# Decoder trunk on one core: the FFN up product with tokens stationary, its result turned by VectorE transposes and SBUF-to-SBUF DMAs

## The chip, the cores and the metric

One core of a Trainium2 chip. The metric is the device time of one execution in microseconds; the time before is the median of three runs.

## The reference

Two layers of a decoder trunk over 256 tokens and 2048 features, float32 throughout. Each layer has a mixer, a cross-attention and a gated convolutional FFN:

```
def conv_ffn(h, w_up, conv_w, conv_b, w_down):
    u = causal_dwconv(h @ w_up, conv_w) + conv_b
    g, val = jnp.split(u, 2, axis=-1)
    return (jax.nn.silu(g) * val) @ w_down

h = h + conv_ffn(rms_norm(h, norm_ffn[l]), ffn_w_up[l], ffn_conv[l], ffn_conv_b[l], ffn_w_down[l])
```

`w_up` is 2048 x 11264, the convolution is causal along the tokens with three taps per feature, `w_down` is 5632 x 2048. The change is in `h @ w_up` and in what reads it.

## The kernel before

Activations lie with features on the 128 partitions and tokens along the free axis. A float32 product is made of three passes of shortened parts: an operand x is held as a rounded part and the exact rest, `x[:, k % 2, 0, :]` and `x[:, k % 2, 1, :]`, and so are the weights; rounded times rounded, rounded times rest and rest times rounded are added up in PSUM.

Weights come in pieces of 128 x 1024 floats (`stream`, L142 to L157). SP's queue issues the load of a piece (`raw`, 4 slots), ACT rounds it (`wh`, L154), DVE subtracts to get the rest (`wl`, L155). `wh` and `wl` have 3 slots each (pool `wp`), so ACT can round a piece when PE has left the one three before it. All loads stand in SP's queue in the order of use. The scheduler of the language sets each engine's order; the instructions inside `high_priority` are moved ahead.

`wstat` (L159) keeps weights stationary. Per k and tile of 128 features it makes one matmul of 512 columns (rounded weights against both parts of x, side by side) and one of 256 (rest of the weights against the rounded part). A call for 256 features fills one PSUM tile of two banks (pool `pmm`, 2 tiles). `xstat` (L178) keeps tokens stationary: per k and block of 128 tokens three matmuls of 512 weight columns. Before the change it serves the mixer's token-major products and the value product of cross-attention (tile `vp`, L187 to L189).

`ffn_up` (L892) runs 44 calls of `wstat`, 256 features each: 128 of the gate and 128 of the value. Each result goes through `ffn_tile` (L876): `fold` adds the two halves (an ACT copy at L201, a DVE addition at L202), `by_row` multiplies with the row factor of the RMSNorm (L206), then per half one ACT scaling with bias (L885) and two DVE multiply-adds along the tokens for the convolution (L886, L887), SiLU (L888), the product (L889), and the split into rounded part and rest (L209, L210). The 22 operand tiles then feed the down product (tile `res`, `project_residual`, L725).

Of the kernel before, what the change touches and what calls it, by code (L numbers as in the profile page):

```python
# [47 lines left out]
# pieces of the main stream between dependent pieces of a background task  # L48
# [15 lines left out]
class Task:  # L64
    """Work cut into pieces, to be emitted between the products of the main stream."""
# [5 lines left out]
class Trunk:  # L71
    def __init__(self, ctx, tc, a):
        self.tc, self.nc, self.a = tc, tc.nc, a
        pool = lambda name, bufs, **kw: ctx.enter_context(tc.tile_pool(name=name, bufs=bufs, **kw))
        self.const = pool("const", 1)
        self.par = pool("par", 1)
        self.actp = pool("actp", 29)
        self.raw = pool("raw", 4)
        self.wp = pool("wp", 3)
        self.tmp = pool("tmp", 6)  # L80
        self.ev = pool("ev", 3)
        self.col = pool("col", 3)
        self.rb = pool("rb", 2)
        self.pmm = pool("pmm", 2, space=bass.MemoryType.PSUM)
        self.psm = pool("psm", 4, space=bass.MemoryType.PSUM)

        self.tasks = deque()

# [6 lines left out]
    def pump(self):  # L95
        """One piece of the first task that isn't waiting."""
        free = None
        for task in self.tasks:
            if not all(t.done for t in task.after):
                continue  # L100
            if task.wait > 0:
                task.wait -= 1
            elif free is None:
                free = task
        if free is not None:
            try:
                free.wait = (next(free.gen) or 1) - 1
            except StopIteration:
                free.done = True
                self.tasks.remove(free)  # L110
# [24 lines left out]
    def claim(self, *tiles):  # L135
        """Slots are given in the order of first writes: these tiles get theirs now."""
        for t in tiles:
            t = t.bitcast(F32) if t.dtype == F32R else t
            self.nc.gpsimd.memset(t[0:32, 0, 0:1] if len(t.shape) == 3 else t[0:32, 0, 0, 0:1], 0.0)

# [1 line left out]
    def stream(self, wd, gc, kt):  # L142
        """Weight pieces from DRAM, split into a rounded part and an exact rest."""
        nc = self.nc
        kp = 1024 // gc
        for k in range(kt):
            if k % kp == 0:
                n = min(kp, kt - k) * gc
                raw = self.raw.tile([P, 1024], F32, tag="raw", name="raw")
                wh = self.wp.tile([P, 1024], F32R, tag="wh", name="wh")  # L150
                wl = self.wp.tile([P, 1024], F32R, tag="wl", name="wl")
                nc.sync.dma_start(raw[:, :n], wd[:, k * gc:k * gc + n])
                with self.tc.high_priority(offset=WPRIO):
                    nc.scalar.copy(wh[:, :n], raw[:, :n])  # L154
                    nc.vector.tensor_tensor(wl[:, :n], raw[:, :n], wh.bitcast(F32)[:, :n], ALU.subtract)  # L155
            o = (k % kp) * gc
            yield k, wh[:, o:o + gc], wl[:, o:o + gc]  # L157

    def wstat(self, xs, wd, kt=KT, name="mm", n=2):  # L159
        """Weights stationary, n output tiles: [A|B] each, A+B the product."""  # L160
        nc = self.nc
        ps = self.pmm.tile([P, 2, 512], F32, tag="mm", name=name)
        for k, wh, wl in self.stream(wd, n * P, kt):
            x = xs(k // 2) if callable(xs) else xs[k // 2]
            xhl = x[:, k % 2, :, :].rearrange("p a t -> p (a t)")
            xh = x[:, k % 2, 0, :]
            for m in range(n):
                ms = slice(m * P, (m + 1) * P)
                if k < kt - 1:
                    nc.tensor.matmul(ps[:, m, :], lhsT=wh[:, ms], rhs=xhl, start=(k == 0), stop=False)  # L170
                    nc.tensor.matmul(ps[:, m, 0:T], lhsT=wl[:, ms], rhs=xh, start=False, stop=False)  # L171
                else:
                    nc.tensor.matmul(ps[:, m, 0:T], lhsT=wl[:, ms], rhs=xh, start=False, stop=False)
                    nc.tensor.matmul(ps[:, m, :], lhsT=wh[:, ms], rhs=xhl, start=False, stop=True)  # L174
            self.pump()
        return ps

    def xstat(self, xs, wd, gc=512, name="mm"):  # L178
        """Tokens stationary: [token block, gc] for both token blocks."""
        nc = self.nc  # L180
        ps = self.pmm.tile([P, 2, 512], F32, tag="mm", name=name)
        for k, wh, wl in self.stream(wd, gc, KT):
            x = xs(k // 2) if callable(xs) else xs[k // 2]
            for tb in range(2):
                ts = slice(tb * P, (tb + 1) * P)
                xh, xl = x[:, k % 2, 0, ts], x[:, k % 2, 1, ts]
                nc.tensor.matmul(ps[:, tb, :gc], lhsT=xh, rhs=wh, start=(k == 0), stop=False)  # L187
                nc.tensor.matmul(ps[:, tb, :gc], lhsT=xh, rhs=wl, start=False, stop=False)  # L188
                nc.tensor.matmul(ps[:, tb, :gc], lhsT=xl, rhs=wh, start=False, stop=(k == KT - 1))  # L189
                self.pump()  # L190
        return ps

# [1 line left out]
    def fold(self, ps, name="z", z=None):  # L194
        """A + B of two output tiles, in SBUF float32."""
# [21 lines left out]
    def prep(self, src, gcol, j, x):  # L217
        """Operand tile of gain * src; the row factor is applied to the products."""
# [8 lines left out]
    def squares(self, src, j, acc):  # L227
        """acc += the squares of a tile"""
# [10 lines left out]
    def rsqrt_cols(self, ss, n, scale, out):  # L239
        """out = 1 / sqrt(ss * scale + EPS): a bit estimate for the scaled sum, and two third-order steps  # L240
        y * (t * t - 10/3 * t + 5) with t = v * y * y, each 8/3 times the root; the scale takes that back."""
# [14 lines left out]
    def spread(self, ps, col):  # L256
        """Every partition of ps gets the column as a row."""
        self.nc.tensor.matmul(ps, lhsT=col.broadcast_to([P, P]), rhs=self.ident, start=True, stop=True)

    def row_factor(self, acc, name, wait=1, *after):  # L260
        """1 / rms of every token, as columns and as a row on every partition; ready when the task is done."""
# [108 lines left out]
    def gla(self, l, tok, kq, ready, o_sb):  # L370
        """Gated linear attention into o_sb [P value, head, T], normalised per head and token."""
# [31 lines left out]
        # scores between tokens s and t by the smallest aligned block that holds both, its middle  # L403
        # between them: the decay is split there, so that every exponent is at most 0
# [23 lines left out]
        def products(lv, ke, qe):  # L428
            """Of a level only the tokens t in the second halves of its blocks are taken."""
# [22 lines left out]
        # blocks of 128 and 256 tokens: keys carried to the end of their chunk, queries from the start  # L452
        # of theirs; over 256 also past the chunk that lies between
# [48 lines left out]
        # values by token, RMSNorm over the value dimension, features back on the partitions  # L502
# [30 lines left out]
    def rope(self, dst, src, cols, tb, n):  # L533
        """dst = rotated src * factor; n heads of 64, cols = (factor, -factor)."""
# [12 lines left out]
    def swa_keys(self, tok, kp, vp):  # L547
        """Keys, and values for the two key heads, each with the other head's half at zero."""
# [35 lines left out]
    def swa(self, g, n, qTs, kp, vp, out):  # L584
        """Eight heads, one block of tokens: tiles j of heads (4g + j, 8 + 4g + j); two operand tiles."""
# [120 lines left out]
    def gla_out(self, o_sb, zr, oa):  # L706
        """Operand of silu(zr) * o."""
# [7 lines left out]
    def conv(self, j, cc, ch, y):  # L715
        """Short convolution of the gated channels (without the output gate)."""
# [8 lines left out]
    def project_residual(self, xs, w, gcol, kt=KT, last=False):  # L725
        """h += product; the operand of the next stage follows tile by tile."""
# [22 lines left out]
    def memory_factor(self):  # L749
        """1 / rms of every memory token, as columns and as a row on every partition."""  # L750
# [126 lines left out]
    def ffn_tile(self, ps, j, rbc, x):  # L877
        nc = self.nc
        z = self.fold(ps)
        self.by_row(z, rbc)  # L880
# [11 lines left out]
    def ffn_up(self, l, xs, acc):  # L892
        out, wait = [], []
        _, rbc, rt = self.row_factor(acc, "rx", W["ss"])
        for j in range(FT):
            wait.append((self.wstat(xs, self.a["wu"][l, j], name="up"), j))
            if j == 0:
                continue
            self.until(rt)
            for ps, i in wait:  # L900
                if i % 2 == 0:
                    out.append(self.operand(f"a{i // 2}"))
                self.ffn_tile(ps, i, rbc, out[-1])
            wait = []
# [26 lines left out]
def _groups(w, gc):  # L931
    """[depth, K, N] -> [depth, N/gc, 128, (K/128) * gc]"""
# [5 lines left out]
def _fm(x):  # L938
    """[256, 2048] -> [8, 128, 2, 256], features on partitions"""
# [3 lines left out]
def _colmajor(v):  # L943
    """[..., n*128] -> [..., 128, n]"""
# [3 lines left out]
def _layout(inp):  # L948
# [21 lines left out]
    d["wu"] = _groups(inp["ffn_w_up"][:, :, pair], 256)  # L970
# [50 lines left out]
```

## Time and profile before

| | |
|---|---|
| median of 3 runs | 2933.92 us (2933.08 to 2934.96) |
| the profiled execution, first to last instruction | 2931.9 us |
| PE, DVE, ACT busy in it | 2902.8, 1941.1, 1503.1 us |
| up product of layer 0, first and last matmul start | 724.6 and 1222.3 us |
| granted clock of TensorE, mean | 0.997 of 2.4 GHz |

The profile shows one execution, with a span of 2931.9 us from its first to its last instruction; the runs' times also hold what lies around it and are 1.2 to 3.1 us longer. Times in the rows are microseconds from the span's start unless marked ns. PE is the matmul, PEld the load of the stationary operand, which runs beside it; a matmul's end is modelled, so the distance from start to start tells its cost. SPq is SP's queue, which only issues DMAs.

### The profile page before, as it was taken

The page shows a single profiled execution, that of the slowest core. Times are in us where ns is not written, and L with a number is a line of the kernel's source. Part 1 is how long each engine was busy: PE and PEld are TensorE (multiplying, and loading weights), DVE is VectorE, ACT ScalarE, POOL GpSimd, SP SyncE. Part 2 cuts the span into 40 slices and gives each one's busy share as a digit, 9 for nine tenths or more (in the row PEclk, how much of TensorE's full clock was granted, in tenths as well). Part 3 has the DMA queues.
Part 4 walks back from the last instruction along what each step waited for, and adds up shares of the span by engine and source line. Part 5 has one row for each costly group of instructions (what it writes and reads, how often), then busy time and mean ns, then how long its engine had stood idle before and what let it go on. Part 6 is the DMA issues. An engine that isn't in the chain of part 4 may idle for free.

```text
span 2931.9 us, 42865 instructions
## 1 busy us (share of the span) xinstructions
PE 2902.8 (99%) x16712; PEld 2523.1 (86%) x16712; DVE 1941.1 (66%) x2865; ACT 1503.1 (51%) x2117; POOL 28.6 (1%) x53
## 2 busy tenths in 40 slices
PE   7999999999999999999999999999999999999998
PEld 7888888888888888888898888888888888888887
DVE  7886665556777777655567866655567777776454
ACT  5565444444555555544455654444455555555443
POOL 3000000000000000000000000000000000000000
PEclk9999999999999999999999999999999999999999
DMA  6556565556556565666664566555555555566664
GB/s 193 156 172 207 189 186 167 165 171 187 184 184 189 184 188 186 191 187 190 183 182 144 166 193 188 186 162 169 174 186 186 187 185 189 184 189 188 188 187 144
DMA packets 148589, 530.32 MB, mean 181 GB/s; under 512 B 17152, under 2 KB 17696, under 8 KB 148384
## 3 DMA queue, kind: packets, MB, share of 16 engines
q1 hardware_dynamic: 148384, 527.57, 58.6%
q8 instruction: 131, 2.15, 0.3%
q14 instruction: 74, 0.61, 0.1%
HBM read 525.40 MB, written 2.10 MB: 180 GB/s over the span
## 4 chain that ended last, share of the span: by engine, by line
PE 98%; DVE 1%; issue 0%; DMA 0%; ACT 0%; SPq 0%; DVEq 0%; ACTq 0%
PE up L170 21%; PE res L170 19%; PE up L171 11%; PE res L171 9%; PE kp L170 4%; PE qp L170 4%; PE vp L188 2%; PE vp L187 2%; PE vp L189 2%; PE qp L171 2%; PE kp L171 2%; PE zc L170 2%; PE up L174 1%; PE zq L187 1%; PE zq L189 1%; PE zq L188 1%
## 5 line engine op out<-in xcount | busy, mean ns | idle before, releaser
L155 DVE TENSOR_TENSOR wl<-raw,wh 128x1024 fp32r<-128x1024 f32 (+2 forms) x993 | 1208.5, 1218 | 720.6 <-ACT wh L154 719.0
L154 ACT CAST wh<-raw 128x1024 fp32r<-128x1024 f32 (+2 forms) x993 | 1033.6, 1041 | 962.1 <-PE res L170 303.0
L170 PE MATMUL up<-xs,wh 128*128 128x512 f32 x2640 | 936.0, 398 | 0.0
L171 PE MATMUL up<-xs,wl 128*128 128x256 f32 x2640 | 741.9, 281 | 0.0
L170 PEld LDWEIGHTS up<-xs,wh 128*128 128x128 f32 x2640 | 496.1, 188 | 118.0
L171 PEld LDWEIGHTS up<-xs,wl 128*128 128x128 f32 x2640 | 498.8, 189 | 3.6
L170 PE MATMUL res<-a,wh 128*128 128x512 f32 x1376 | 482.6, 395 | 0.0
L171 PE MATMUL res<-a,wl 128*128 128x256 f32 x1376 | 385.9, 280 | 0.0
L170 PEld LDWEIGHTS res<-a,wh 128*128 128x128 f32 x1376 | 258.0, 187 | 60.1
L171 PEld LDWEIGHTS res<-a,wl 128*128 128x128 f32 x1376 | 260.0, 189 | 0.8
L170 PE MATMUL qp<-xs,wh 128*128 128x512 f32 x480 | 171.4, 397 | 0.0
L170 PE MATMUL res<-xo,wh 128*128 128x512 f32 x480 | 170.5, 398 | 0.0
L170 PE MATMUL kp<-ms,wh 128*128 128x512 f32 x480 | 169.5, 397 | 0.0
L171 PE MATMUL res<-xo,wl 128*128 128x256 f32 x480 | 134.9, 281 | 0.0
L171 PE MATMUL qp<-xs,wl 128*128 128x256 f32 x480 | 134.8, 281 | 0.0
L171 PE MATMUL kp<-ms,wl 128*128 128x256 f32 x480 | 134.6, 280 | 0.0
L201 ACT COPY z_b<-up 128x512 f32<-128x512 f32 x88 | 51.6, 587 | 161.3 <-PE up L174 161.3
L202 DVE TENSOR_TENSOR z<-up,z_b 128x512 f32<-128x512 f32 x88 | 60.9, 692 | 105.8 <-ACT z_b L201 105.8
L885 ACT ACTIVATE u<-z,par 128x256 f32<-128x256 f32 x176 | 96.6, 595 | 48.7 <-DVE z L206 48.7
L170 PEld LDWEIGHTS res<-xo,wh 128*128 128x128 f32 x480 | 90.2, 188 | 21.3
L170 PEld LDWEIGHTS kp<-ms,wh 128*128 128x128 f32 x480 | 90.1, 188 | 21.1
L170 PEld LDWEIGHTS qp<-xs,wh 128*128 128x128 f32 x480 | 90.1, 188 | 18.9
(316 smaller groups left out, 4145.3 us busy)
## 6 DMA issues: line engine op xcount, KB each, us to landing
raw<-in_wu SPq DMA_DIRECT2D x352, 512.0 KB, 4.5
raw<-in_wd SPq DMA_DIRECT2D x175, 512.0 KB, 3.6
raw<-in_w_fm SPq DMA_DIRECT2D x80, 512.0 KB, 4.3
raw<-in_wk SPq DMA_DIRECT2D x64, 512.0 KB, 4.8
raw<-in_wo SPq DMA_DIRECT2D x64, 512.0 KB, 4.4
raw<-in_wq SPq DMA_DIRECT2D x64, 512.0 KB, 4.0
raw<-in_wv SPq DMA_DIRECT2D x64, 512.0 KB, 3.6
raw<-in_wxo SPq DMA_DIRECT2D x64, 512.0 KB, 3.9
```

Source lines behind the costliest of these rows:

```text
L154: nc.scalar.copy(wh[:, :n], raw[:, :n])
L155: nc.vector.tensor_tensor(wl[:, :n], raw[:, :n], wh.bitcast(F32)[:, :n], ALU.subtract)
L170: nc.tensor.matmul(ps[:, m, :], lhsT=wh[:, ms], rhs=xhl, start=(k == 0), stop=False)
L171: nc.tensor.matmul(ps[:, m, 0:T], lhsT=wl[:, ms], rhs=xh, start=False, stop=False)
L174: nc.tensor.matmul(ps[:, m, :], lhsT=wh[:, ms], rhs=xhl, start=False, stop=True)
L187: nc.tensor.matmul(ps[:, tb, :gc], lhsT=xh, rhs=wh, start=(k == 0), stop=False)
L188: nc.tensor.matmul(ps[:, tb, :gc], lhsT=xh, rhs=wl, start=False, stop=False)
L189: nc.tensor.matmul(ps[:, tb, :gc], lhsT=xl, rhs=wh, start=False, stop=(k == KT - 1))
L201: nc.scalar.copy(b, ps[:, :, T:2 * T])
L202: nc.vector.tensor_tensor(z, ps[:, :, 0:T], b, ALU.add)
L885: nc.scalar.activation(u[:, s, :], z[:, s, :], AF.Identity, bias=self.p[:, C_FB + m:C_FB + m + 1], scale=tap[2])
```

## The change

`ffn_up` calls `xstat` instead of `wstat`, 512 features (two pairs of gate and value tiles) at a time: 22 calls a layer. With `striped=True` the stationary operand takes every second token, so that block tb holds tokens 2m + tb, and its elements lie 8 bytes apart. The result then has tokens on the partitions, and the new `turn` brings features back there: for each block a DVE transpose of 32 x 32 squares from PSUM into `zt`, then 16 DMAs of 32 partitions x 1 KB from `zt` to `zf`, all issued by SP. The row factor is multiplied in one DVE instruction of 1024 elements per partition that reads `zf` and writes back to `zt`; `fold` and `by_row` are no longer called here. `zt` and `zf` have two slots each; the scratch for dynamic DMAs is set to 1024, and `w_up` is laid out in groups of 512 columns.

```diff
+        self.turnp = pool("turnp", 2)
...
-    def xstat(self, xs, wd, gc=512, name="mm"):
+    def xstat(self, xs, wd, gc=512, name="mm", kt=KT, striped=False):
...
+                if striped:
+                    xh, xl = (x[:, k % 2, u, :].rearrange("p (m b) -> p b m", b=2)[:, tb, :] for u in range(2))
+                else:
+                    xh, xl = (x[:, k % 2, u, tb * P:(tb + 1) * P] for u in range(2))
...
+    def turn(self, ps, name="z"):
+        nc = self.nc
+        zt = self.turnp.tile([P, 4, 4, 32, 2], F32, tag="zt", name=name + "_t")
+        zf = self.turnp.tile([P, 4, 4, 64], F32, tag="zf", name=name)
+        with self.tc.high_priority(offset=WPRIO):
+            for tb in range(2):
+                nc.vector.transpose(out=zt[:, :, :, :, tb].rearrange("p b k j -> p k b j"),
+                                    in_=ps[:, tb, :].rearrange("p (k b j) -> p k b j", k=4, b=4))
+            for a in range(4):
+                for b in range(4):
+                    nc.sync.dma_start(zf[32 * b:32 * b + 32, a].rearrange("p k u -> p (k u)"),
+                                      zt[32 * a:32 * a + 32, b].rearrange("p k j t -> p (k j t)"))
+        return zf, zt.rearrange("p b k j t -> p (b k j t)").rearrange("p (k t) -> p k t", k=4)
...
-    def ffn_tile(self, ps, j, rbc, x):
-        nc = self.nc
-        z = self.fold(ps)
-        self.by_row(z, rbc)
+    def ffn_tile(self, z, j, x):
+        nc = self.nc
...
-        for j in range(FT):
-            wait.append((self.wstat(xs, self.a["wu"][l, j], name="up"), j))
+        for j in range(0, FT, 2):
+            zf, z = self.turn(self.xstat(xs, self.a["wu"][l, j // 2], name="up", striped=True))
             if j == 0:
-                continue
-            self.until(rt)
+                self.until(rt)
+            nc.vector.tensor_tensor(z.rearrange("p k (a u) -> p k a u", a=4), zf.rearrange("p a k u -> p k a u"),
+                                    rbc.rearrange("p (a u) -> p a u", a=4).unsqueeze(1).broadcast_to([P, 4, 4, 64]),
+                                    ALU.mult)
+            out.append(self.operand(f"a{j // 2}"))
+            for i in range(2):
+                self.ffn_tile(z[:, 2 * i:2 * i + 2], j + i, out[-1])
```

The order on DVE in the middle of the up product. Before, one group of 256 features (four pieces; `wl` is the rest of a weight piece, `z` the folded result, `u` the convolution, `a` the operand of the down product):

```order
L202 TENSOR_TENSOR z<-up,z_b 128x512
L206 TENSOR_TENSOR z<-z,rxb 128x512
L155 TENSOR_TENSOR wl<-raw,wh 128x1024
L886 SCALAR_TENSOR_TENSOR u<-z,par,u 128x255 x2
L887 SCALAR_TENSOR_TENSOR u<-z,par,u 128x254 x2
L155 TENSOR_TENSOR wl<-raw,wh 128x1024
L889 TENSOR_TENSOR u<-u 128x256
L155 TENSOR_TENSOR wl<-raw,wh 128x1024
L210 TENSOR_TENSOR a_8095<-u,a_8095 128x256
L155 TENSOR_TENSOR wl<-raw,wh 128x1024
```

Now, from one turn on, one group of 512 features (eight pieces; `z_t` is `zt`, `z` is `zf`):

```order
L206 STREAM_TRANSPOSE z_t<-up 128x4x4x32 x2
L156 TENSOR_TENSOR wl<-raw,wh 128x1024 x4
L919 TENSOR_TENSOR z_t<-z,rxb 128x1024
L905 SCALAR_TENSOR_TENSOR u<-z_t,par,u 128x255 x2
L906 SCALAR_TENSOR_TENSOR u<-z_t,par,u 128x254
L905 SCALAR_TENSOR_TENSOR u<-z_t,par,u 128x255
L906 SCALAR_TENSOR_TENSOR u<-z_t,par,u 128x254
L905 SCALAR_TENSOR_TENSOR u<-z_t,par,u 128x255
L906 SCALAR_TENSOR_TENSOR u<-z_t,par,u 128x254
L156 TENSOR_TENSOR wl<-raw,wh 128x1024
L906 SCALAR_TENSOR_TENSOR u<-z_t,par,u 128x254
L156 TENSOR_TENSOR wl<-raw,wh 128x1024
```

The transposes stand right after the group's end, four rests of weight pieces follow, and then the row product, which waits for the 16 DMAs; seven multiply-adds stand between it and the next rest. The pieces of these rests, counted from the first of the finished group: 10 to 13 before the row product, 14 behind the seventh multiply-add.

The order in SP's queue at the head of layer 0's up product. Before:

```order
L152 DMA raw<-in_wv 128x1024 x32
L152 DMA raw<-in_wxo 128x1024 x32
L152 DMA raw<-in_wu 128x1024 x176
L152 DMA raw<-in_wd 128x1024 x82
L152 DMA raw<-in_wd 128x512
```

Now:

```order
L153 DMA raw<-in_wxo 128x1024 x32
L153 DMA raw<-in_wu 128x1024 x14
L210 DMA z<-z_t 32x256 x16
L153 DMA raw<-in_wu 128x1024 x8
L210 DMA z<-z_t 32x256 x16
L153 DMA raw<-in_wu 128x1024 x8
L210 DMA z<-z_t 32x256 x16
```

The 16 DMAs of a turn stand between the weight loads of pieces 13 and 14, counted as above; what SP issues behind them waits until they are issued.

## Rows read from the trace of the kernel before

**Rows 1.** The page's engines: busy us (share of the span) xinstructions.
```profile
PE 2902.8 (99%) x16712; PEld 2523.1 (86%) x16712; DVE 1941.1 (66%) x2865; ACT 1503.1 (51%) x2117; POOL 28.6 (1%) x53
```

**Rows 2.** The page's chain that ended last: shares of the span by engine.
```profile
PE 98%; DVE 1%; issue 0%; DMA 0%; ACT 0%; SPq 0%; DVEq 0%; ACTq 0%
```

**Rows 3.** Tile up, layer 0: duration ns min/median/max, first to last start us.
```profile
L170 PE MATMUL up<-xs,wh x1320: 387/398/481, 724.6 to 1221.5; 128*128 128x512 f32 x189
...
L174 PE MATMUL up<-xs,wh x88: 392/394/400, 735.8 to 1222.3; 128*128 128x512 f32 x88
```

**Rows 4.** Timeline of PE, a group's end: start us, duration us, instruction.
```profile
905.93 0.39 PE L174 MATMUL up<-xs,wh 128*128 128x512 f32 x1
906.16 0.39 PE L170 MATMUL up<-xs,wh 128*128 128x512 f32 x1
```

**Rows 5.** Timeline of ACT, the same group and the next; idle time before in brackets.
```profile
906.36 0.59 ACT L201 COPY z_b<-up 128x512 f32<-128x512 f32 x1 [1.90 <-PE up L174]
...
908.43 1.10 ACT L885 ACTIVATE u<-z,par 128x256 f32<-128x256 f32 x2 [0.54 <-DVE z L206]
...
917.66 0.59 ACT L201 COPY z_b<-up 128x512 f32<-128x512 f32 x1 [1.90 <-PE up L174]
```

**Rows 6.** Timeline of DVE, the same group.
```profile
907.70 0.69 DVE L206 TENSOR_TENSOR z<-z,rxb 128x512 f32<-128x512 f32 x1
908.31 1.22 DVE L155 TENSOR_TENSOR wl<-raw,wh 128x1024 fp32r<-128x1024 f32 x1
909.45 0.87 DVE L886 SCALAR_TENSOR_TENSOR u<-z,par,u 128x255 f32<-128x255 f32 x2
```

**Rows 7.** Timeline of PE in the value product, tokens stationary.
```profile
533.13 0.40 PE L188 MATMUL vp<-wl,ms 128*128 128x512 f32 x1
...
534.96 0.39 PE L187 MATMUL vp<-wh,ms 128*128 128x512 f32 x1
```

**Rows 8.** Timeline of ACT in the value product: first and last of four roundings.
```profile
571.31 1.05 ACT L154 CAST wh<-raw 128x1024 fp32r<-128x1024 f32 x1 [1.67 <-PE vp L189]
...
579.47 1.05 ACT L154 CAST wh<-raw 128x1024 fp32r<-128x1024 f32 x1 [1.67 <-PE vp L189]
```

**Rows 9.** Groups by line and shape, 747 to 1224 us: busy us, mean ns | idle before.
```profile
L155 DVE TENSOR_TENSOR wl<-raw,wh 128x1024 fp32r<-128x1024 f32 x169 | 206.3, 1221 | 70.4 <-ACT wh L154 70.4
L154 ACT CAST wh<-raw 128x1024 fp32r<-128x1024 f32 x169 | 176.9, 1047 | 89.6 <-PE up L170 89.6
L885 ACT ACTIVATE u<-z,par 128x256 f32<-128x256 f32 x84 | 46.1, 596 | 22.4 <-DVE z L206 22.4
```

**Rows 10.** Groups by line and shape on DVE, whole span.
```profile
L809 DVE TENSOR_REDUCE xac<-xs 128x2 f32<-128x512 f32 x8 | 5.5, 692 | 3.9 <-PE xs L803 3.9
...
L500 DVE COPY am<-att 64x512 f32<-64x512 f32 x2 | 0.8, 421 | 0.1
```

**Rows 11.** Timeline of SP's queue at the start: issues without a wait.
```profile
0.74 0.39 SPq L297 DMA_DIRECT2D gmix<-in_gmix  x1
...
2.12 0.43 SPq L152 DMA_DIRECT2D raw<-in_w_tok  x1
2.60 0.43 SPq L304 DMA_DIRECT2D h<-in_x  x1
...
4.02 0.43 SPq L152 DMA_DIRECT2D raw<-in_w_tok  x1
```

**Rows 12.** DMA issues: xcount, KB each, median us from issue to landing.
```profile
raw<-in_wu SPq DMA_DIRECT2D x352, 512.0 KB, 4.5
...
gmix<-in_gmix SPq DMA_DIRECT2D x1, 8.0 KB, 1.8
```

**Rows 13.** Tile out (256 KB each, SBUF to DRAM at the end): its DMAs.
```profile
DMA to landing us min/median/max: 2.0/2.4/2.6
```

**Rows 14.** Windows: stretch, us, busy us by engine, granted clock, DMA share, GB/s.
```profile
747.00:1224.00 477.00, 477.00 (x2704) 414.27 (x2703) 353.33 (x508) 270.04 (x381) 0.00 (x0) 1.00 0.60 187
```

**Rows 15.** Loads of the stationary operand in the value product, whole span.
```profile
L187 PEld LDWEIGHTS vp<-wh,ms 128*128 128x128 f32 x256 | 48.1, 188 | 9.4
```

More of the change, by code (lines that the diff above doesn't have):

```diff
@@ L176, in wstat @@
         return ps
-    def xstat(self, xs, wd, gc=512, name="mm"):
+    def xstat(self, xs, wd, gc=512, name="mm", kt=KT, striped=False):
         nc = self.nc
         ps = self.pmm.tile([P, 2, 512], F32, tag="mm", name=name)
-        for k, wh, wl in self.stream(wd, gc, KT):
+        for k, wh, wl in self.stream(wd, gc, kt):
             x = xs(k // 2) if callable(xs) else xs[k // 2]
             for tb in range(2):
-                ts = slice(tb * P, (tb + 1) * P)
-                xh, xl = x[:, k % 2, 0, ts], x[:, k % 2, 1, ts]
+                if striped:
+                    xh, xl = (x[:, k % 2, u, :].rearrange("p (m b) -> p b m", b=2)[:, tb, :] for u in range(2))
+                else:
+                    xh, xl = (x[:, k % 2, u, tb * P:(tb + 1) * P] for u in range(2))
                 nc.tensor.matmul(ps[:, tb, :gc], lhsT=xh, rhs=wh, start=(k == 0), stop=False)
                 nc.tensor.matmul(ps[:, tb, :gc], lhsT=xh, rhs=wl, start=False, stop=False)
-                nc.tensor.matmul(ps[:, tb, :gc], lhsT=xl, rhs=wh, start=False, stop=(k == KT - 1))
+                nc.tensor.matmul(ps[:, tb, :gc], lhsT=xl, rhs=wh, start=False, stop=(k == kt - 1))
                 self.pump()
         return ps
+    def turn(self, ps, name="z"):
[11 more added lines that the diff above has]
+        return zf, zt.rearrange("p b k j t -> p (b k j t)").rearrange("p (k t) -> p k t", k=4)
     def fold(self, ps, name="z", z=None):
@@ L892, in ffn_up @@
     def ffn_up(self, l, xs, acc):
-        out, wait = [], []
+        nc = self.nc
+        out = []
         _, rbc, rt = self.row_factor(acc, "rx", W["ss"])
-        for j in range(FT):
-            wait.append((self.wstat(xs, self.a["wu"][l, j], name="up"), j))
+        for j in range(0, FT, 2):
+            zf, z = self.turn(self.xstat(xs, self.a["wu"][l, j // 2], name="up", striped=True))
             if j == 0:
-                continue
-            self.until(rt)
[L900 to L904, printed above, removed]
+                self.until(rt)
[5 more added lines that the diff above has]
+                self.ffn_tile(z[:, 2 * i:2 * i + 2], j + i, out[-1])
         return out
@@ L969, in _layout @@
     pair = np.arange(2 * D_FF).reshape(2, FT, P).transpose(1, 0, 2).reshape(-1)
-    d["wu"] = _groups(inp["ffn_w_up"][:, :, pair], 256)
+    d["wu"] = _groups(inp["ffn_w_up"][:, :, pair], 512)
     d["x"], d["mem"] = _fm(inp["x"][0]), _fm(inp["mem"][0])
@@ L1009 @@
     arrays = _layout({n: np.asarray(v) for n, v in inputs.items()})
-    nc = bacc.Bacc("TRN2", target_bir_lowering=False, num_devices=1)
+    nc = bacc.Bacc("TRN2", target_bir_lowering=False, num_devices=1, dynamic_dma_scratch_size=1024)
     feeds, aps = {}, {}
```

## Prediction

> **What bounds the kernel now.** Read the engines' busy time first: TensorE (PE) is busy 99% of the span, VectorE (DVE) 66%, ScalarE (ACT) 51% [rows 1]. The chain of waits says the same: 98% of it is PE [rows 2]. So time can be won only by giving PE less to do, and lost by making it wait. The up product runs from 724.6 us to just after 1222.3 in layer 0 [rows 3] and as long in layer 1. Its group of 256 features ends every 11.30 us: ACT's copy of a finished group starts at 906.36 and the next at 917.66 [rows 5]. 44 groups take 44 x 11.30 = 497.2 us a layer. PE doesn't pause between groups [rows 4]; in the stretch DVE works 353 of 477 us and the DMA engines are busy 0.60 [rows 14], so both have room on average.
>
> **PE's own work.** The columns don't change: for 512 features and one k, 4 pairs of 512 + 256 before, 6 matmuls of 512 after, 3072 columns both times. The number of matmuls falls from 8 to 6, and each has a price of its own. The nearest rows of the new form are the value product of cross-attention, the same helper with tokens stationary: 8 matmuls start in 534.96 - 533.13 = 1.83 us [rows 7], and where nothing else is mixed in, a weight piece of two k (12 matmuls) takes (579.47 - 571.31) / 3 = 2.72 us [rows 8], 0.227 a matmul. Before, the same piece took 11.30 / 4 = 2.83 us. After: 22 groups x 8 pieces x 2.72 = 478.7 us a layer, 18.5 less; two layers give **-37 us**, if PE never waits.
>
> **What is taken off and put on beside PE.** Off, per 512 features: two ACT copies, two DVE folds and two row products (the last cost DVE 0.69 each in the timeline [rows 6]). On: two transposes out of PSUM, one product of 1024 elements, 16 DMAs on SP's queue. The taps, SiLU and splits stay. DVE's average load hardly moves, so I price none of this as throughput. What counts is the order in which DVE, ACT and SP wait.
>
> **The chain behind each turn.** Let t = 0 be the moment a group's last matmul gives way to the next (906.16 in [rows 4]); ACT follows 0.20 later [rows 5]. Call the finished group's pieces 0 to 7. There are three slots for the rounded part and three for the rest, so piece n is rounded only when PE has left piece n-3. DVE's order after the change is: two transposes, the rests of pieces 10 to 13, the row product, seven of the eight multiply-adds, the rest of piece 14. Two things must be there before the row product.
>
> - The rest of piece 13. PE leaves piece 10 at 3 x 2.72 = 8.16; +0.20, +1.05 for the rounding [rows 9], and 0.04 to hand over, as from DVE to ACT in [rows 5, 6]: it starts at 9.45. DVE's next instruction follows 1.14 later (908.31 to 909.45 [rows 6]): **10.59**.
> - The sixteenth DMA. No row shows a transpose. A read of 512 columns of PSUM by a one-source instruction took 692 ns, a copy of 512 in SBUF 421 ns [rows 10]; above, two passes would be 1.38 us. I take 0.69, as that row reads the same amount from the same memory. The second starts 0.61 after the first, as behind the 0.69 of [rows 6]; both are done at 0.20 + 0.61 + 0.69 = 1.50. SP's queue issues one DMA every (4.02 - 2.12) / 4 = 0.475 us when nothing holds it [rows 11]: the sixteenth starts at 1.55 + 15 x 0.475 = 8.67. No row shows a transfer from SBUF to SBUF. The nearest, 8 KB into an idle queue and 256 KB out of SBUF, land 1.8 and at least 2.0 us after issue [rows 12, 13]; 4.5 us, the weights' own time among each other [rows 12], is the upper end. I take 2.05, since by then SP has issued no weights for 8 us: 10.7, and with eight semaphores to pass **10.85**.
>
> So the row product starts at about 10.85 and ends 1.22 later (1024 elements, as the row of the same size [rows 9]), at 12.07. Then ACT starts 0.04 later and needs 0.60 for the first of four scalings and 0.51 for each further one [rows 5, 9], a multiply-add holds DVE 0.40 (two in 0.87 us [rows 6]). In the order given the seventh starts 3.15 after the product's end, piece 14's rest at 3.55, and it is there at 4.77: 16.84. PE wants it with its second matmul of piece 14, at 6 x 2.72 + 0.23 = 16.55; with 0.1 to hand over, **PE waits 0.4 us per group**. Without any late DMA it would be 0.1. The wait repeats after every group but the last of a layer, whose followers are the slower pieces of the down product: 42 x 0.4 = 17 us.
>
> The weights queued behind the 16 DMAs on SP have cover: piece 14 is issued at 8.67 + 0.475 = 9.15 and lands by 13.7 [rows 12], its rounding is due at 14.2. The start and the end of the stage cost nothing: the last operand of the down product is wanted only at its k = 42, some 29 us later.
>
> **A rule weighed against a row.** SP's row shows 0.43 us per issue and 0.475 from one to the next [rows 11], so 16 issues are 7.6 us and they are what makes the product late. The Trainium skill, DMA: Bandwidth & Descriptors, "Anatomy of one DMA", puts the sequencer's dispatch at about 50 ns, though for the GpSimd path. By that the sixteen would be out in an estimated 0.8 us, nothing would be late, and the time would be that of the second case below; I go by the row.
>
> **Sum.** -37 + 17 = **-20 us**. The profiled execution spans 2931.9 us, 2 below the median of the runs, 2933.9; from the median: **2914 us**.
>
> **The cases.** About 0.2% (6 us) is what a measurement of this kernel can tell from no change.
>
> 1. Forecast, the product 0.1 to 0.6 late: 2903 to 2928, chance 0.40.
> 2. Nothing late: transposes near 0.42, or a shorter issue for 32 partitions. For it: 16 transfers of 32 KB are small. Against: an issue of 8 KB holds SP 0.39 us, one of 256 KB 0.43 [rows 11]. -37 + 42 x 0.12 = -32: 2902, chance 0.18.
> 3. **A wait takes the place of the work removed, and more.** The place is DVE's row product, with piece 14's rest queued behind it. Each microsecond that it starts later costs PE 42 us. It decides against the change when the product starts after about 11.35 (a wait of 0.88 x 42 = 37). Transposes of 1.38 us put it at 12.2: 42 x 1.8 - 37 = +37, 2971. Landing at 3.2 instead of 2.05 puts it at 12.0: +28, 2962. For it: the spare time is under 0.5 us, and two unpriced operations stand in series. Against: each nearest row is well under these ends. Chance 0.34, a third of it within 0.2%.
> 4. **The stationary load becomes PE's pace.** Tokens are now taken every second element, 8 bytes apart. The packed load took 188 ns [rows 15], hidden under 227 ns. It decides from 227 ns: each further ns costs 4224 matmuls 4.2 us, and twice 188 would cost 4224 x 0.149 = +630 us. No row has a load with such a step. The Trainium skill, SBUF — State Buffer, "Door 1: The DMA port swizzle", says SBUF is read in lines of 16 bytes at full rate as long as two accesses fall in a line; a step of 8 bytes is just that, so by it this case doesn't come. No run here shows it. Chance 0.08.
>
> **How the numbers follow.** The likeliest is case 1. Cases 1 and 2 are faster, 0.57 with a little of the first lost to the middle; within 0.2% comes the middle of case 3, 0.12; slower 0.31. The range reaches from 2896, no wait at all, to 2965 in case 3; outside lie the ends of cases 3 and 4. Cases 1 and 2 alone would span 2896 to 2928.
>
> **What would show it.** In the changed profile: up matmuls 0.227 us apart and stationary loads at 188 ns (else case 4); sixteen SP issues spread over 7 us after each pair of transposes; the row product starting about 10.85 us after a group's end; one gap of some 0.4 us in PE per group, released by DVE's rest of the seventh piece of the next group. No gap means case 2; a gap over 0.88 makes the prediction's sign wrong. If the gap is released by ACT's rounding waiting for a weight DMA instead, the queue's cover was misjudged.

## The result, and the profile after

The changed kernel takes **3099.22 us** (3094.78 to 3100.68), against 2933.82 for the kernel before on the same chip: a ratio of 1.0562, 95% interval 1.055 to 1.0575. The forecast was 2914 with a range to 2965: the change costs time where a gain was expected, and the time lies 134 us above the range.

The profile of the changed kernel, its engines (answers to [rows 1]) and the chain that ended last (answers to [rows 2]), by engine and by line:

```profile
PE 2967.7 (96%) x15304; PEld 2508.6 (81%) x15304; DVE 1941.0 (63%) x2821; ACT 1450.8 (47%) x2029; POOL 29.3 (1%) x53
...
PE 70%; SPq 13%; DVE 9%; DMA 4%; issue 3%; ACT 1%; DVEq 0%; ACTq 0%
PE res L171 17%; SPq L210 13%; PE res L172 9%; PE kp L171 4%; PE qp L171 4%; PE up L192 3%; PE up L191 3%; PE up L193 3%; DVE wl L156 2%; DMA z<-z_t 2%; DVE u L905 2%; PE vp L192 2%; PE vp L191 2%; PE vp L193 2%; PE qp L172 2%
```

The chain was 98% PE and is now 70%. The largest share that isn't PE's is line 210 in SP's queue: issuing the turn's DMAs, 13%.

One group's end as the timeline shows it (start us, duration us, instruction, idle time before). Its last matmul starts at 901.39, so t = 0 of the prediction is 901.62. First SP's queue, then DVE, then ACT:

```profile
903.16 10.24 SPq L210 DMA_DIRECT2D z<-z_t  x16
913.50 14.52 SPq L153 DMA_DIRECT2D raw<-in_wu  x8
```

```profile
901.82 1.31 DVE L206 STREAM_TRANSPOSE z_t<-up 128x512 f32<-128x512 f32 x2
...
911.07 1.23 DVE L156 TENSOR_TENSOR wl<-raw,wh 128x1024 fp32r<-128x1024 f32 x1 [1.57 <-ACT wh L155]
914.87 1.23 DVE L919 TENSOR_TENSOR z_t<-z,rxb 128x1024 f32<-128x1024 f32 x1 [2.57 <-DMA z<-z_t]
...
919.63 1.22 DVE L156 TENSOR_TENSOR wl<-raw,wh 128x1024 fp32r<-128x1024 f32 x1
```

```profile
916.13 2.08 ACT L904 ACTIVATE u<-z_t,par 128x256 f32<-128x256 f32 x4 [5.09 <-DVE z_t L919]
918.12 1.98 ACT L155 CAST wh<-raw 128x1024 fp32r<-128x1024 f32 x2
```

The transposes start at 0.20 and are done at 1.51, SP issues from 1.54, the last of the 16 leaves at about 11.2, and the row product starts at 13.25 instead of 10.85. Behind it stand ACT's four scalings and two roundings, and on DVE the rest at 919.63. PE meets both (timeline of PE):

```profile
917.96 0.40 PE L193 MATMUL up<-wh,xs 128*128 128x512 f32 x1
919.20 0.51 PE L191 MATMUL up<-wh,xs 128*128 128x512 f32 x1 [0.84 <-ACT wh L155]
920.90 0.51 PE L192 MATMUL up<-wl,xs 128*128 128x512 f32 x1 [1.20 <-DVE wl L156]
...
922.09 0.63 PE L193 MATMUL up<-wh,xs 128*128 128x512 f32 x1
922.52 0.63 PE L191 MATMUL up<-wh,xs 128*128 128x512 f32 x1
```

Two matmuls start 1.24 and 1.70 us after the one ahead of them instead of 0.23, so PE loses 2.5 us. Then something comes that the prediction doesn't have: matmuls 0.43 us apart. The windows show why (stretch, its us, busy us of PE, PEld, DVE, ACT and POOL, granted clock, DMA share, GB/s):

```profile
747.00:1224.00 477.00, 438.91 (x1768) 351.95 (x1767) 305.67 (x419) 213.85 (x293) 0.00 (x0) 0.96 0.55 181
902.00:915.00 13.00, 13.00 (x58) 10.74 (x57) 6.05 (x7) 4.06 (x4) 0.00 (x0) 1.00 0.36 102
...
921.70:925.10 3.40, 3.40 (x10) 2.61 (x9) 3.24 (x6) 0.81 (x2) 0.00 (x0) 0.51 0.83 198
925.20:932.00 6.80, 6.80 (x31) 5.64 (x30) 3.65 (x4) 3.14 (x3) 0.00 (x0) 1.00 0.62 214
```

For 3.4 us behind the gap the granted clock is at its lower level, 1.2 GHz. The same stretch of the kernel before has 1.00 and no idle PE [rows 14].

The matmuls and the stationary loads of the up product (ns min/median/max, first and last start) answer to [rows 3] and [rows 15]:

```profile
L191 PEld LDWEIGHTS up<-wh,xs x1408: 192/193/334, 723.4 to 2832.2; 128*128 128x128 f32 x176
L191 PE MATMUL up<-wh,xs x1408: 389/394/632, 723.6 to 2832.4; 128*128 128x512 f32 x176
...
L206 DVE STREAM_TRANSPOSE z_t<-up x88: 673/696/720, 747.2 to 2834.0; 128x512 f32<-128x512 f32 x88
```

Sorted by the distance from one up matmul's start to the next: what is over 0.7 us is a gap (less the 0.23 of its own), what lies between 0.3 and 0.7 is called a short distance (again less 0.23), the rest is PE's own pace. Of both layers together, in us:

| | before | changed |
|---|---|---|
| PE's own pace | 994.4 | 985.2 |
| gaps | 0 | 117.0 |
| short distances | 1.4 | 53.8 |

Of the 53.8 us, 48.0 lie in stretches for which the trace has 1.2 GHz; the other 5.8 are short waits. -9.2 + 117.0 + 52.4 = +160.2 of the 166.8 us by which the span grew (3098.7 - 2931.9); the rest lies outside the up product.

### The profile page after: what moved, and what is told of

It is laid out like the page before. It is cut to its first block, busy times and chain, and to the rows that moved or that the text cites. A ratio compares the mean times of both kernels' runs of the same rounds, so it can differ in the third digit from the quotient of the medians.

```text
span 3098.7 us, 40756 instructions
## 1 busy us (share of the span) xinstructions
PE 2967.7 (96%) x15304; PEld 2508.6 (81%) x15304; DVE 1941.0 (63%) x2821; ACT 1450.8 (47%) x2029; POOL 29.3 (1%) x53
## 4 chain that ended last, share of the span: by engine, by line
PE 70%; SPq 13%; DVE 9%; DMA 4%; issue 3%; ACT 1%; DVEq 0%; ACTq 0%
PE res L171 17%; SPq L210 13%; PE res L172 9%; PE kp L171 4%; PE qp L171 4%; PE up L192 3%; PE up L191 3%; PE up L193 3%; DVE wl L156 2%; DMA z<-z_t 2%; DVE u L905 2%; PE vp L192 2%; PE vp L191 2%; PE vp L193 2%; PE qp L172 2%
## 5 line engine op out<-in xcount | busy, mean ns | idle before, releaser
L156 DVE TENSOR_TENSOR wl<-raw,wh 128x1024 fp32r<-128x1024 f32 (+2 forms) x993 | 1206.3, 1215 | 813.1 <-ACT wh L155 809.7
L192 PE MATMUL up<-wl,xs 128*128 128x512 f32 x1408 | 578.5, 411 | 48.2 <-DVE wl L156 48.2
L191 PE MATMUL up<-wh,xs 128*128 128x512 f32 x1408 | 571.7, 411 | 50.1 <-ACT wh L155 50.1
L193 PE MATMUL up<-wh,xs 128*128 128x512 f32 x1408 | 574.3, 408 | 0.0
L191 PEld LDWEIGHTS up<-wh,xs 128*128 128x128 f32 x1408 | 285.0, 202 | 127.9 <-ACT wh L155 68.4
L192 PEld LDWEIGHTS up<-wl,xs 128*128 128x128 f32 x1408 | 282.6, 201 | 120.2 <-DVE wl L156 61.3
L193 PEld LDWEIGHTS up<-wh,xs 128*128 128x128 f32 x1408 | 283.0, 201 | 58.3
L904 ACT ACTIVATE u<-z_t,par 128x256 f32<-128x256 f32 x176 | 91.5, 590 | 235.1 <-DVE z_t L919 235.1
L919 DVE TENSOR_TENSOR z_t<-z,rxb 128x1024 f32<-128x1024 f32 x44 | 53.9, 1225 | 124.2 <-DMA z<-z_t 111.3
```

What stands on the lines that cost most here:

```text
L904: nc.scalar.activation(u[:, s, :], z[:, s, :], AF.Identity, bias=self.p[:, C_FB + m:C_FB + m + 1], scale=tap[2])
L919: nc.vector.tensor_tensor(z.rearrange("p k (a u) -> p k a u", a=4), zf.rearrange("p a k u -> p k a u"), rbc.rearrange("p (a u) -> p a u", ...
```

## The experiments

All are made from the changed kernel. The first theory is that SP's issue time makes the product late; its rivals lie in the 32-partition transfers, in DVE's order and in the stationary load. The kernel before took 2932.46 us beside runs 1 to 4 and 2934.17 beside runs 5 to 8. "Gaps", "short distances" and "pace" are sorted as above, for both layers; what of the short distances is the lower clock is said by the clock in the trace. Runs 1 to 8 are one execution each.

### 1. The stationary read packed

```diff
-            ... self.xstat(xs, self.a["wu"][l, j // 2], name="up", striped=True)
+            ... self.xstat(xs, self.a["wu"][l, j // 2], name="up")
```

> The changed kernel, but the stationary operand takes 128 adjacent tokens instead of every second one; everything else, the turn included, is as it was, so the tokens of the FFN's input come out in another order. Theory C, that the 8-byte step costs TensorE: the up matmuls go from 0.233 us apart (changed kernel, between gaps) back to the 0.227 of the value product, the load from 193 to 188 ns, and the span falls by 4224 x 0.0063 = 27 us, from 3098.7 to about 3072; the gaps after each turn stay. Rival, that the wider spacing has another cause (weights arriving, the banks): 0.233 stays and the span with it, 3095 to 3102.

Measured: 3090.1 us. The load takes 188 ns again:

```profile
L191 PEld LDWEIGHTS up<-wh,xs x1408: 186/188/334, 724.8 to 2823.4; 128*128 128x128 f32 x176
```

Pace 961.0 instead of 985.2, 24 us less, near the 27 expected; but the gaps grew to 133.6, and the span fell by 10.6 and not by 27. Most of what PE saves before the seventh piece it spends waiting there, since the product's time hangs on SP and not on PE. So the step of the stationary read has a price, and while there are gaps most of it can't be seen in the time.

### 2. Four DMAs of 128 partitions

```diff
-            for a in range(4):
-                for b in range(4):
-                    nc.sync.dma_start(zf[32 * b:32 * b + 32, a]..., zt[32 * a:32 * a + 32, b]...)
+            for a in range(4):
+                nc.sync.dma_start(zf[:, a]..., zt[:, a]...)
```

> The changed kernel with 4 DMAs of 128 partitions per turn in place of 16 of 32: the same bytes, the same waits, but features are not brought back to their partitions, so the FFN's values are not the reference's. Theory A, the 16 issues in SP's queue make the row product late: four issues end some 2.5 us after the transposes, the row product starts at about 10.6 us after a group's end (behind the rest of piece 13) instead of 13.1, PE's gap falls from 2.3 to 4 us to at most 0.2, the clock stays at its upper level, span about 2931.9 - 9 + 4 = 2927. Theory B, the transposes, the product and the multiply-adds that stand ahead of the next weight piece are too long by themselves: gaps over 1 us stay, span over 3000. By the way: SP's step per issue, 0.633 us for 32 partitions, tells whether it goes with the shape or with the source in SBUF.

Measured: 2930.9 us, granted clock 0.997, no gaps, 2.4 us of short distances and none of them at the lower clock. The same bytes move; the squares aren't brought to their partitions. SP's queue around a group's end:

```profile
908.28 2.42 SPq L209 DMA_DIRECT2D z<-z_t  x4
910.80 18.64 SPq L153 DMA_DIRECT2D raw<-in_wu  x8
```

With 12 issues less, 168 us are gone, so theory B is out. The issues are as far apart as the 16 were (medians of 0.64 and 0.63 us): the longer step is not one of few partitions. Nor is a source in SBUF enough for it. The issues of `out`, SBUF to DRAM at the end of the kernel, hold SP 332 ns each (here in the kernel before), where those of the turn never take less than 507 (here in the changed kernel), though the first of each turn follows a pause:

```profile
L928 SPq DMA_DIRECT2D out<-h x8: 332/332/348, 2924.2 to 2928.5; - x8
```

```profile
L210 SPq DMA_DIRECT2D z<-z_t x704: 507/589/1619, 748.6 to 2844.1; - x176
```

What sets the step, both ends in SBUF, the rows of 1 KB or something else, stays open. And without any gap the time is that of before: PE's pace is 990.8, so with this stationary read the change hardly saves PE anything.

### 3. The product one group later, in the text

```diff
+            if late:
+                finish(*late)
+            late = (j, *turned)
```

> The changed kernel, but the row product and the tile's work of a group are written one group later, so that nothing on DVE waits for the DMAs just issued; the 16 issues still stand in one row in SP's queue. Theory A in its narrow form (only the row product's wait matters): no gap, about 2927. Theory A in its wide form (SP's 10 us also hold up the weights behind them): piece 14's load is issued 11.8 us after a group's end, lands at about 15.5, its rounding and its rest end 2.3 later, at 17.8, where PE wants it at 6 x 2.8 + 0.2 = 17.0: a gap of some 0.8 us per group, released by ACT's rounding that waited for a weight DMA, 42 x 0.8 = 34: about 2960, or some 20 more where the clock falls. Theory B: gaps as before, over 3050.

Measured: 3096.6 us, gaps 116.1, short distances 52.4: no difference. It didn't test what it was meant to, so the time says nothing for theory B either. The scheduler put the product back where it was on DVE, behind the same four rests, with the same wait, 2.57 us. Run 7 below forces it.

### 4. The DMAs spread among PE's work

The edit of run 3 is in this run too; only what is new is shown.

```diff
+    def move(self, zf, zt):
+        for a in range(4):
+            for b in range(4):
+                self.nc.sync.dma_start(zf[32 * b:32 * b + 32, a]..., zt[32 * a:32 * a + 32, b]...)
+                yield 2
```

> As the run with the later product, but the 16 DMAs are written as background pieces between the next group's matmuls; in SP's queue 12 still stand in one row and 4 behind later weight loads. Theory A, wide form: piece 14's load is issued after 12 issues, 1.8 + 12 x 0.633 = 9.4 us after a group's end, and lands at 13.0, in time for a rest that is due at 17.0: no gap, clock at its upper level, 2931.9 - 9 = about 2923. If the gaps stay over 0.5 us, the order of SP's queue is not the cause.

Measured: 3019.2 us, so the expectation was missed. Gaps 55.6, short distances 27.4; no stretch of the up product has the lower clock here, so these are short waits. Twelve of the 16 still stand in a row in SP's queue, and behind them the weights are late. SP's queue:

```profile
919.20 8.27 SPq L213 DMA_DIRECT2D z<-z_t  x12
927.57 0.53 SPq L153 DMA_DIRECT2D raw<-in_wu  x1
```

and ACT, which rounds what SP loads:

```profile
931.48 1.05 ACT L155 CAST wh<-raw 128x1024 fp32r<-128x1024 f32 x1 [6.46 <-DMA raw<-in_wu]
```

So there is a second wait, which the first one had covered: the weight loads queued behind the turn's issues. The product's own wait for the DMAs is down to 32.6 us in all, from 111.3.

### 5. The issues on GpSimd

```diff
-                    nc.sync.dma_start(zf[32 * b:32 * b + 32, a]..., zt[32 * a:32 * a + 32, b]...)
+                    nc.gpsimd.dma_start(zf[32 * b:32 * b + 32, a]..., zt[32 * a:32 * a + 32, b]...)
```

> Edit: the turn's 16 DMAs are issued by GpSimd, which is idle here, and no more by SP; their sizes, tiles and number stay. SP's queue then holds the weight loads alone, and the compiler's order puts the row product eight weight splits later on VectorE. Theory Q (the gaps come from SP's issue time, 16 x 0.63 us, which holds back the product and the weight loads behind it): the gaps of 117 us and the 54 us at the lower clock go, and the time falls to that of the run with four DMAs, 2931, if GpSimd issues 16 in less than a group of 22.6 us. What one issue costs GpSimd no run shows yet: at 0.63 us each there is room, from 1.3 us each GpSimd is itself late and the time would be over 3000. Theory T (16 transfers of 32 partitions disturb the weights' transfers whoever issues them): gaps stay and the time is over 3020.

Measured: 2932.9 us; no gaps, 1.8 us of short distances and none of them at the lower clock. GpSimd's timeline at a group's end; then, of the turned tile, the issues and the time to landing; then the stationary load in tile up:

```profile
907.42 7.93 POOL L210 DMA_DIRECT2D z<-z_t  x16 [14.28 <-DVE z_t L206]
```

```profile
L210 POOL DMA_DIRECT2D z<-z_t x704: 496/496/659, 749.1 to 2679.5; - x176
...
DMA to landing us min/median/max: 1.6/3.7/6.2
```

```profile
L191 PEld LDWEIGHTS up<-wh,xs x1408: 193/197/202, 723.7 to 2668.8; 128*128 128x128 f32 x176
```

The same 16 transfers, landing later than from SP (3.7 us against 1.9; the last one 14 us after the group's end), cost nothing. They go by another DMA queue than SP's (the page of this run has 22528 packets, 704 x 32, under software_dynamic), so what the 16 do from SP's queue is seen in run 7. Here it is not the transfers that cost; it is who waits in which queue. This run takes away both waits at once: SP's queue holds weights alone, and the compiler's order puts the row product behind all but one of the rests up to the next group's end.

### 6. Half of the issues on ScalarE

```diff
-                    nc.sync.dma_start(zf[...
+                    (nc.sync if b % 2 else nc.scalar).dma_start(zf[...
```

> Edit: 8 of the 16 DMAs are issued by ScalarE, 8 by SP. Theory Q: SP's part ends 8 x 0.63 = 5.1 us earlier, so the product could start about 8 us after its group's end instead of 13.1, and with the weight loads 5 us earlier no gap of 2 to 4 us is left; but ScalarE pays 8 x 0.63 = 5.1 us for its own issues in front of weight roundings, each group (47% of its time is busy in the changed kernel, 5.1 of 22.6 us is 23% more), so a rounding can now be late there: between 2931 (ScalarE keeps up) and about 3010 (half of the waits are left). Theory T: over 3020.

Measured: 3100.2 us, above the whole range of theory Q and, by its number, where theory T would have it. Gaps 113.4, short distances 57.2, 48.1 of them at the lower clock. DVE, then ACT and its queue, then PE:

```profile
904.36 1.19 DVE L156 TENSOR_TENSOR wl<-raw,wh 128x1024 fp32r<-128x1024 f32 x1
911.95 1.23 DVE L919 TENSOR_TENSOR z_t<-z,rxb 128x1024 f32<-128x1024 f32 x1 [6.40 <-DMA z<-z_t]
913.09 3.49 DVE L156 TENSOR_TENSOR wl<-raw,wh 128x1024 fp32r<-128x1024 f32 x3
```

```profile
904.47 6.00 ACTq L210 DMA_DIRECT2D z<-z_t  x8
910.57 2.94 ACT L155 CAST wh<-raw 128x1024 fp32r<-128x1024 f32 x3 [6.39 <-DMA z<-z_t]
```

```profile
911.67 0.51 PE L191 MATMUL up<-wh,xs 128*128 128x512 f32 x1 [0.18 <-ACT wh L155]
914.37 0.50 PE L192 MATMUL up<-wl,xs 128*128 128x512 f32 x1 [2.19 <-DVE wl L156]
```

The DMAs are indeed out 5 us earlier, and the product starts 8 to 9 us after the group's end. But the compiler's order now puts it behind one rest and no more behind four, so DVE stands for 6.4 us in front of it, ACT as long behind its own issues, and the gap is at the fourth piece instead of the seventh. The number alone doesn't decide between the theories; by the lines, theory Q's range was wrong because it assumed that the product stays where it was. Two things are late here, and the run doesn't part them cleanly. PE waits 0.35 us for the rounding behind ACT's issues and then 2.5 us for the rest behind the product. Without the product in front, an estimate from these lines, that rest could have started when the first rounding ended, at 911.62 instead of 913.09: about half of the gap goes with ACT's own issues, half with the product's place. So landing 5 us earlier gains nothing here: ACT pays for it with its issues, and less of DVE's work stands ahead of the instruction that waits.

### 7. The product forced behind the next group's transposes

The edit of run 3 and the split of the product into four instructions are in this run too; only the forced order is shown.

```diff
+                one = self.cols("one", 1)
+                nc.vector.tensor_scalar(one, turned[1][:, 0, 0:1], 0.0, 1.0, ALU.mult, ALU.add)
+                finish(*late, one)
```

> Edit: the row product of a group takes a factor 1 that is written from the next group's turned values, so that VectorE cannot run it before the next group's transposes; it is then four scalar_tensor_tensor of 256 columns. SP still issues the 16 DMAs in a row ahead of the weight loads. This separates the two waits. If the product's wait (VectorE and ScalarE held in their queues until the 16th DMA lands) is all: no gaps, 2930 to 2940. If the weight loads behind SP's 16 issues are late as well (16 x 0.633 = 10.1 us in which no weights are asked for): gaps stay, released by a weight's DMA, at pieces later than the 7th of a group, and the time is between 2960 and 3030.

Measured: 2984.0 us, inside the second range. Gaps 48.7; short distances 9.3, which are short waits, since no stretch of the up product has the lower clock. The product's wait for the DMAs is gone (1.5 us in all, against 111.3). What is left, in SP's queue, in ACT's timeline, and in the list of waits (us in total, times, longest):

```profile
901.73 11.67 SPq L153 DMA_DIRECT2D raw<-in_wu  x8
```

```profile
905.50 1.05 ACT L155 CAST wh<-raw 128x1024 fp32r<-128x1024 f32 x1 [3.71 <-DMA raw<-in_wu]
```

```profile
ACT wh L155 <- DMA raw<-in_wu: 202.7, 124, 6.5
```

The load that is issued at 901.73, right behind the 16, is rounded from 905.50, 3.8 us later, and in this run the loads of `w_up` land 4.5 us after their issue in the median, as before [rows 12]. So the load is late by its issue; the 16 transfers from SP don't make the loads slower. Two parts of the loss come apart: of the gaps of 117.0, 48.7 stay when only the weights wait behind SP's issues, and 68.3 go with the product's wait, and with them the stretches at the lower clock. (One thing was expected wrongly: these gaps are at the same piece, the seventh, not later.)

### 8. GpSimd's issues and a packed stationary

```diff
-        zt = self.turnp.tile([P, 4, 4, 32, 2], F32, tag="zt", name=name + "_t")
+        zt = self.turnp.tile([P, 4, 4, 2, 32], F32, tag="zt", name=name + "_t")
...
-            zf, z = self.turn(self.xstat(xs, self.a["wu"][l, j // 2], name="up", striped=True))
+            zf, z = self.turn(self.xstat(xs, self.a["wu"][l, j // 2], name="up"))
```

The transposes write to the new layout, the row product is done in two halves, one per token block, and line 210 is as in run 5.

> Edit: as the run with GpSimd's issues, and the stationary is read packed (128 tokens in a row) instead of every second token; the token blocks then lie one after the other in the turned tile, and the row product is done in two halves. Theory Q with the load's step as a cost of its own: without gaps the PE time of a layer is that of the packed run, 480.5 us against 497.2 before, so 33 us less in two layers: 2895 to 2902. If 2925 or more, the saving of the packed load is lost elsewhere; over 3000 if GpSimd's issues are late.

Measured: 2898.9 us. Engines, and the load:

```profile
PE 2868.8 (99%) x15304; PEld 2455.3 (85%) x15304; DVE 1932.5 (67%) x2865; ACT 1452.1 (50%) x2029; POOL 373.1 (13%) x757
```

```profile
L191 PEld LDWEIGHTS up<-wh,xs x1408: 187/188/192, 725.5 to 2634.6; 128*128 128x128 f32 x176
```

A layer's up product takes 479.7 us, of which 478.8 are pace. The span is 35.0 below that of before.

### 9. and 10. Runs 8 and 5, timed

> The packed stationary with GpSimd's issues again, timed: the one look gave 2898.9 against 2934.2 on the same chip, so 2899 and a ratio of 0.988. If the saving had come with that one execution, the median would lie nearer to 2931.

> GpSimd's issues with the stationary as the change reads it (every second token), timed: the one look gave 2932.9 against 2934.2. Theory Q with the load's step as a cost of its own: the step takes back what the saved matmul columns give, 497.4 us per layer against 497.2 before, so no difference from before that can be told: 2929 to 2937, and 33 to 37 us above the packed run of this call.

Measured beside 2933.68 us for the kernel before: the packed one **2898.24 us**, ratio 0.9878 (0.9863 to 0.9894); the one with every second token 2933.07 us, ratio 0.9999 (0.999 to 1.0007). The first beats both kernels of this case; between the two lie 35 us, the step of the stationary read and the layout that goes with it.

## Why the prediction was wrong, step by step

- **What bounds the kernel, and the place of the wait: right.** One gap per group, at the seventh piece of the next group, released by DVE's rest of that piece and, which the prediction left out, by ACT's rounding of it, both queued behind the row product.
- **The chain behind the turn up to SP: right.** Transposes 0.696 us (taken: 0.69), done at 1.51 (1.50), first issue at 1.54 (1.55). The landing is right too, 1.85 in the median (2.05), and the product, 1.23 (1.22); from the last landing to the product 0.22 to 0.39 us pass (0.13 was added, from no row). In five groups of layer 1, though, a landing of up to 4.1 us put the product at 14.5 to 15.0.
- **SP's issue step failed: 0.475 was taken, 0.63 to 0.64 was measured.** In the group shown the 16 take 10.24 us, so the sixteenth starts at about 11.2 instead of 8.67, and the product at 13.25 instead of 10.85. The rows were of loads from DRAM [rows 11], and for these the step still holds: the weight loads right behind the 16 are again 0.47 us apart (914.12, 914.59, 915.07). An issue from SBUF to SBUF costs more, whatever the number of partitions (run 2); why stays open. The prediction's own rule then gives the gaps: 2.4 us later and the 0.4 it had, 42 x 2.8 = 118 us; measured 117.0. That it is so near is partly luck: over the 42 groups the product starts at 13.0 to 15.0, 13.5 in the mean, by which the rule gives 129, and PE's slower pace makes it want the piece 72 x 0.0066 = 0.5 us later. The price itself holds: from group to group, each microsecond that the product starts later goes with 0.95 us more of gap. So case 3 came, by its mechanism and its price per microsecond, but through a term that the prediction had read from a row and not bounded. The rule of the Trainium skill that was weighed there (DMA: Bandwidth & Descriptors, "Anatomy of one DMA", about 50 ns of dispatch) is not what sets the pace here: 0.63 us from SP, and still some 0.5 from GpSimd, the path for which the page gives it (run 5).
- **SP's cover failed: "The weights queued behind the 16 DMAs on SP have cover".** With the measured step the loads stand 10.2 us behind the turn, and on their own they cost 48.7 us of gaps (run 7). In the changed kernel this lies inside the same gaps.
- **The -37 us was mis-sized: -9** (-4 in run 2 and none in run 5, which have no gaps). The price per matmul was right for a packed operand: 478.7 us a layer were worked out, 478.8 measured (run 8). But the prediction held the load to be hidden up to 227 ns. It isn't: the load's 188, 193 and 197 ns go with 0.227, 0.233 and 0.2355 us from matmul to matmul (runs 8, changed kernel, 5), so here a nanosecond of load cost PE about a nanosecond. In case 4 the mechanism was there, without the threshold. The Trainium skill, TensorE: Matmul & The Clock Gate, "Back-to-back issue gap", says that load and matmul both set the distance in such a stream; these rows agree. The rule of the Trainium skill from SBUF — State Buffer, "Door 1: The DMA port swizzle", by which a step of 8 bytes is free, doesn't hold here: 5 to 9 ns in 188.
- **A term was missing: the clock.** Behind about two of three gaps TensorE was granted 1.2 GHz for some 3.4 us, which cost 48.0 us in all. The prediction counted a wait once.

Put together: the sum with the measured step, -37 + 118, would have been +81 and the sign right; the load's step adds 28, the clock 48 and short waits 6, together +163, of 165.4 between the medians.

## What to carry to other kernels

A DMA is priced by its issue in the queue that issues it, and by what stands behind it there; take the step from a row of the same kind of transfer, and give even a step that has a row bounds when it is multiplied by 15. An instruction that waits for a DMA holds everything behind it on its engine, so look in the compiled order how much of other work stands ahead of it, and move small, many-fold DMAs to an engine that has nothing else to do. When PE runs one load per matmul without a pause, the load is part of PE's pace, and its read pattern counts.

## What was not expected of the hardware

- From SP, a DMA from SBUF to SBUF is issued every 0.63 to 0.64 us (16 in 10.24, four in 2.42), one from DRAM every 0.475, and one from SBUF to DRAM holds SP 0.33 us. GpSimd issues the same 16 in 7.93 us, about 0.5 each, and they land after 3.7 us instead of 1.9; DVE's rests are not slower meanwhile (1218 ns against 1215).
- A stationary operand read with a step of 8 bytes loads in 193 ns, and in 196 to 198 in run 5 and in the first layer of run 2; packed it is 188. In the second layer of run 2, without gaps too, it is 193 again; what makes the difference stays open.
- Gaps of 2.1 to 4.3 us per group were followed in two of three groups by about 3.4 us at 1.2 GHz, so that a microsecond of gap cost some 0.4 us more. In runs 4 and 7, with gaps of about 1 us per group, no such stretch came in the up product. Why some long gaps have none stays open; no run was made for it.
